# Attention scores: the low part of the rotated queries as 64-row products, two banks of keys side by side

## The chip, the core and the metric

The kernel runs on one core of one Trainium2 chip. The metric is the device time of one execution in microseconds (us). A core has five engines with a queue of their own: TensorE (PE in the profile; its weight loads are listed apart as PEld), VectorE (DVE), ScalarE (ACT), GpSimd (POOL) and SyncE (SP, which issues most DMAs). Products land in PSUM, eight banks of 512 fp32 values on each of 128 partitions.

## The reference

One layer of a hybrid backbone on 2048 latent and 256 context tokens: an input projection feeds latent attention, a bidirectional HGRN2 scan and Fourier mixing; then come an output projection and a SwiGLU FFN. The change is in the attention scores. With absorbed weights, a score of query t and key s is the sum of a 128-long product with the compressed keys and a 64-long product of the rotated parts:

```
q_nope, q_pe = q[..., :MLA_NOPE], q[..., MLA_NOPE:]        # 128 and 64 columns
q_pe = apply_rope(q_pe, rope[0], rope[1])
k = jnp.concatenate([k_nope, jnp.broadcast_to(k_pe, (b, t, MLA_HEADS, MLA_ROPE))], axis=-1)
s = jnp.einsum('bqhd,bkhd->bhqk', qi, k).astype(jnp.float32) * scale
pr = jax.nn.softmax(s, axis=-1).astype(v.dtype)
```

There are 4 heads and 2304 keys.

## The kernel before

Precision is kept by splitting each fp32 operand into a high part (rounded to fp32r, the type that TensorE streams fast) and a low part (the rest). `hi` writes the first, `lo` the second, and `mm3` makes low times high, high times high and high times low in one PSUM bank.

The attention stage lies between about 977 and 1764 us of the span. `group` runs over 4 blocks of 512 queries, 4 heads and 2 halves. One group scores two tiles of 128 queries (I call one such tile with its 2304 keys a unit: 64 units in all) while it gathers the values of the group before: `turn` transposes probabilities (tile `ptv`), ACT and DVE split them into `pth` and `ptl`, and `gather` multiplies them with the compressed keys into `po`. `score_bank(u, j)` makes the scores of 512 keys (256 in the fifth bank, j = 4) in a PSUM tile `sc`, of which there are five. Five products go into each bank:

- `ktl` and `kth` with `q[0]`, and `kth` with `q[1]`: the compressed part, on 128 rows of the array;
- `kp` with `q[2]` and `kp` with `q[3]`: the rotated part. Rows 0 to 63 and 64 to 127 of `q[2]` hold the same 64 rotated values (high part), those of `q[3]` the same low part. `kp` holds the keys' high part on rows 0 to 63 and their low part on rows 64 to 127, so that one 128-row product gives high times both parts.

DVE then takes the maximum of the bank (L890), after the fifth bank the maximum of all (L893), and ACT takes the five exponentials (L896), which free the banks for the next unit. A scheduler sets the order on each engine when the kernel is built; the engines run their queues in that order.

Two other places in the program use a part of the array at a time, and the prediction reads them. In `hgrn` products into `pfin` (L408, L410) use 32 or 64 columns of the array at a `tile_position`. At the start the modulation rows are transposed (L212) with 2 rows, which the compiler places on a tile of 32 rows by 128 columns, and L215 follows on the full array.

Of the kernel before, what the change touches and what calls it, by code (L numbers as in the profile page):

```python
# [14 lines left out]
ALU = mybir.AluOpType  # L15
AX = mybir.AxisListType
# [3 lines left out]
P = 128  # L20
# [4 lines left out]
NTOK = SEQ + CTX  # L25
# [17 lines left out]
def tile_backbone(  # L43
# [6 lines left out]
    pe, act, dve, pool, sp = nc.tensor, nc.scalar, nc.vector, nc.gpsimd, nc.sync  # L50
# [19 lines left out]
    def hi(eng, dst, src):  # L70
        if eng is pool:
            pool.tensor_scalar(dst, src, 1.0, 0.0, ALU.mult, ALU.add)  # L72
        elif eng is act:
            act.copy(dst, src)  # L74
        else:
            dve.tensor_copy(dst, src)

    def lo(dst, src, h, eng=None):
        (eng or dve).tensor_tensor(dst, src, h, ALU.subtract)  # L79
# [548 lines left out]
    with ExitStack() as ph:  # L628
# [16 lines left out]
        kth = cp.tile([P, NTOK], F32R, name="kth")  # L645
        ktl = cp.tile([P, NTOK], F32R, name="ktl")
        kp = cp.tile([P, NTOK], F32R, name="kp")

        def keys(g):

            kv = qp2.tile([P, 2, 256], F32, tag=f"q{g // 2 % 4}", name="kv")
            sp.dma_start(kv, mlap[g // 4][(g % 4) * P:(g % 4 + 2) * P, 256:512].rearrange("(c p) n -> p c n", p=P))
            hi(act, ckh[:, g:g + 2, :], kv[:, :, 0:128])
            lo(ckl[:, g:g + 2, :], kv[:, :, 0:128], ckh[:, g:g + 2, :], pool)
            pt = ps1.tile([P, 512], F32, tag=f"p{'ab'[g // 2 % 2]}{g // 4 % 2}", name="ptk")
            for s in range(2):
                for i in range(2):
                    pe.transpose(pt[:, (2 * s + i) * P:(2 * s + i + 1) * P], kv[:, i, s * P:(s + 1) * P], ident)
            gs = slice(g * P, (g + 2) * P)
            hi(act, kth[:, gs], pt[:, 0:256])  # L660
            lo(ktl[:, gs], pt[:, 0:256], kth[:, gs])
            hi(act, kp[:, gs], pt[:, 256:512])
            lo(kp[64:P, gs], pt[64:P, 256:512], kp[64:P, gs])

        def queries(b):

# [55 lines left out]
        with ExitStack() as early:  # L722
# [34 lines left out]
            for g in (16, 0, 2, 4, 6, 8, 10, 12, 14):  # L757
                keys(g)
# [117 lines left out]
        def score_bank(u, j):  # L876

            q, t = u["q"], u["t"]
            ts = slice(t * P, (t + 1) * P)
            js = slice(j * 512, min((j + 1) * 512, NTOK))  # L880
            n = js.stop - js.start
            if j == 0:
                u["mx"] = rp.tile([P, 16], F32, tag="mx", bufs=4, name="mx")
                u["p"] = b4.tile([P, NTOK], F32, tag="p", name="p")
                u["s"] = []
            s = pss.tile([P, 512], F32, tag="sc", name="sc")
            for i, (a, bb) in enumerate(((q[0], ktl), (q[0], kth), (q[1], kth), (q[2], kp), (q[3], kp))):
                pe.matmul(s[:, :n], a[:, ts], bb[:, js], start=i == 0, stop=i == 4)  # L888
            mx = u["mx"]
            dve.tensor_reduce(mx[:, j:j + 1], s[:, :n], AX.X, ALU.max)  # L890
            u["s"].append(s)
            if j == 4:
                dve.tensor_reduce(mx[:, 5:6], mx[:, 0:5], AX.X, ALU.max, negate=True)  # L893
                for i in range(5):
                    a, e = i * 512, min((i + 1) * 512, NTOK)
                    act.activation(u["p"][:, a:e], u["s"][i][:, :e - a], AF.Exp, bias=mx[:, 5:6],  # L896
                                   accum_out=mx[:, 6 + i:7 + i])
# [78 lines left out]
        def group(cur, prev, tasks):  # L976

            turned = [None] * 9
            for i in range(9 + LAG):
                values = [lambda: gather(prev["po"], prev["g"] * 256, i - LAG, turned[i - LAG])]  # L980
                if prev is None or i < LAG:
                    values = []
                if prev is not None and i < 9:
                    turned[i] = turn(prev["u"], i)
                scores = [lambda: score_bank(cur["u"][i // 5], i % 5)] if cur is not None and i < 10 else []
                for f in values + scores if i % 5 == 0 else scores + values:
                    f()
                if prev is not None and prev["g"] == 1 and i == 3:
                    weights(prev)
                if tasks and i < 10:  # L990
                    more = tasks.pop(0)()
                    if more is not None:
                        tasks.insert(min(2, len(tasks)), more)
            if cur is not None:
                for u in cur["u"]:
                    dve.tensor_reduce(cur["rc"][:, u["t"]:u["t"] + 1], u["mx"][:, 6:11], AX.X, ALU.add)
                if cur["g"] == 1:
                    dve.reciprocal(cur["rc"], cur["rc"])
            if prev is not None and prev["g"] == 1:
                tasks.insert(min(2, len(tasks)), finish(prev["b"], prev["h"], prev["po"], prev["rb"]))  # L1000
# [37 lines left out]
    with ExitStack() as ph:  # L1038
# [90 lines left out]
        gs = ph.enter_context(ExitStack())  # L1129
# [66 lines left out]
        def token_sums(s, k, eng):  # L1196

            raw = raw4("xr")
            for i in range(4):
                sp.dma_start(raw[:, i, :], x2d[s][i][k * P:(k + 1) * P, :])  # L1200
            t = st.tile([P, 3, TB], F32, tag="ws", name="ts")
            block_sums(eng, [raw[:, i, :] for i in range(4)], [t[:, 0, :], t[:, 1, :]], False)
            return raw[:, 0, :], (t[:, 0, :], t[:, 1, :], raw[:, 1, :], raw[:, 2, :])
# [93 lines left out]
        for i, (s, j) in enumerate(units):  # L1297
# [54 lines left out]
            if s == 0 and 2 <= j < 6:  # L1352
                b11, ts = token_sums(1, j - 2, dve)
# [27 lines left out]
        for b in range(NB):  # L1381
            sq = b1.tile([P, 4, 2], F32, tag="sq7", bufs=2, name="sq7")
            rs = b1.tile([P, 4, 2], F32, tag="rs7", bufs=2, name="rs7")
            for c in range(2):
                acc = [bank("dn") for _ in range(4)]
                for g, (k0, nk) in enumerate(DG):
                    i = (b * 2 + c) * len(DG) + g
# [69 lines left out]
```

## Time and profile before

| | |
|---|---|
| time, median of 3 runs | 3330.2 us (3325.0 to 3332.26) |
| profiled execution | 3330.5 us, of which the span is 3328.7 us |
| PE busy | 3167.2 us, 95% of the span, 17034 matmuls |
| DVE, ACT, POOL busy | 2128.5, 951.0, 1029.7 us |
| attention stage (977 to 1764 us) | 787.0 us, PE busy 767.67 us, granted clock 0.99 |

The span runs from the first to the last instruction. Matmuls are pipelined: a row's own duration contains the way through the array, and what one costs in a stream is the distance between the starts of two neighbours.

### The profile page before, as it was taken

The page shows a single profiled execution, that of the slowest core. Times are in us where ns is not written, and L with a number is a line of the kernel's source. Part 1 is how long each engine was busy: PE and PEld are TensorE (multiplying, and loading weights), DVE is VectorE, ACT ScalarE, POOL GpSimd, SP SyncE. Part 2 cuts the span into 40 slices and gives each one's busy share as a digit, 9 for nine tenths or more (in the row PEclk, how much of TensorE's full clock was granted, in tenths as well). Part 3 has the DMA queues.
Part 4 walks back from the last instruction along what each step waited for, and adds up shares of the span by engine and source line. Part 5 has one row for each costly group of instructions (what it writes and reads, how often), then busy time and mean ns, then how long its engine had stood idle before and what let it go on. Part 6 is the DMA issues. An engine that isn't in the chain of part 4 may idle for free. (4 is left out here: it accounts for less than half of the span.)

```text
span 3328.7 us, 45452 instructions
## 1 busy us (share of the span) xinstructions
PE 3167.2 (95%) x17034; PEld 2651.4 (80%) x17034; DVE 2128.5 (64%) x3219; ACT 951.0 (29%) x2028; POOL 1029.7 (31%) x1233
## 2 busy tenths in 40 slices
PE   7998999999889999999999989999999999999998
PEld 5777777777768888888887767888878888888886
DVE  6575665656686767676655467866776666555543
ACT  3323122222335545555552341111121111212111
POOL 3443452424421021121001443333333333243442
PEclk8999999999999999999999999999999999999999
DMA  6523233143361122120106664422342232664552
GB/s 224 170 70 121 81 106 94 55 117 99 117 194 32 45 58 74 52 78 20 52 28 213 232 213 159 139 77 88 109 136 80 77 95 93 211 211 155 177 171 70
DMA packets 354000, 382.03 MB, mean 115 GB/s; under 512 B 46234, under 2 KB 236532, under 8 KB 352756
## 3 DMA queue, kind: packets, MB, share of 16 engines
q1 hardware_dynamic: 339140, 368.11, 35.3%
q10 hardware_dynamic: 13776, 8.92, 0.8%
q8 instruction: 135, 2.21, 0.3%
q0 software_dynamic: 864, 2.10, 0.2%
q14 instruction: 85, 0.70, 0.1%
HBM read 293.33 MB, written 85.72 MB: 114 GB/s over the span
## 5 line engine op out<-in xcount | busy, mean ns | idle before, releaser
L72 POOL TENSOR_SCALAR wp<-wr 128x512 fp32r<-128x512 f32 x208 | 171.3, 837 | 360.9 <-PE dn L85 229.6
L890 DVE TENSOR_REDUCE mx<-sc 128x1 f32<-128x512 f32 (+1 forms) x320 | 201.9, 632 | 121.7 <-PE sc L888 120.8
L85 PE MATMUL dn<-wp,hdl 128*128 128x512 f32 x704 | 274.0, 389 | 0.0
L83 PE MATMUL dn<-wp,hdh 128*128 128x512 f32 x704 | 274.0, 389 | 0.0
L84 PE MATMUL dn<-wp,hdh 128*128 128x512 f32 x704 | 274.0, 389 | 0.0
L79 DVE TENSOR_TENSOR wp<-wr,wp 128x512 fp32r<-128x512 f32 x208 | 171.1, 860 | 138.4 <-POOL wp L72 138.3
L79 DVE TENSOR_TENSOR ptl<-ptv,pth 128x512 fp32r<-128x512 f32 x288 | 196.1, 686 | 67.4 <-ACT pth L74 65.1
L74 ACT CAST pth<-ptv 128x512 fp32r<-128x512 f32 x288 | 169.3, 592 | 239.3 <-PE ptv L904 232.8
L896 ACT ACTIVATE p<-sc,mx 128x512 f32<-128x512 f32 (+1 forms) x320 | 201.6, 648 | 91.0 <-DVE mx L893 87.1
L83 PE MATMUL y<-xol,wp 128*128 128x512 f32 x528 | 208.9, 396 | 12.5 <-ACT e L1309 5.6
L72 POOL TENSOR_SCALAR wp<-wg 128x512 fp32r<-128x512 f32 x176 | 131.7, 749 | 273.5 <-PE y L85 109.5
L84 PE MATMUL y<-xoh,wp 128*128 128x512 f32 x528 | 207.5, 393 | 0.0
L85 PE MATMUL y<-xoh,wp 128*128 128x512 f32 x528 | 206.8, 392 | 0.0
L85 PE MATMUL accf<-xh,wl 128*128 128x512 f32 x448 | 184.8, 412 | 10.4 <-DVE wl L79 10.4
L888 PE MATMUL sc<-kth,q 128*128 128x512 f32 (+1 forms) x640 | 194.5, 377 | 0.0
L79 DVE TENSOR_TENSOR wl<-wraw,wh 128x1536 fp32r<-128x1536 f32 (+3 forms) x78 | 118.6, 1520 | 116.8 <-POOL wh L72 114.0
L888 PE MATMUL sc<-kp,q 128*128 128x512 f32 (+1 forms) x640 | 190.4, 374 | 0.0
L904 PE MATMUL ptv<-ident,p 128*128 128x128 f32 x1152 | 179.5, 275 | 10.2 <-DVE ptl L79 8.7
L83 PE MATMUL accf<-xl,wh 128*128 128x512 f32 x448 | 184.1, 411 | 0.6 <-DVE gt L559 0.5
L79 DVE TENSOR_TENSOR wp<-wg,wp 128x512 fp32r<-128x512 f32 x176 | 129.3, 737 | 86.2 <-POOL wp L72 82.8
L84 PE MATMUL accf<-xh,wh 128*128 128x512 f32 x448 | 183.0, 408 | 0.0
L72 POOL TENSOR_SCALAR wp<-ws 128x512 fp32r<-128x512 f32 x132 | 90.2, 683 | 286.5 <-PE z L85 160.4
(366 smaller groups left out, 8415.0 us busy)
## 6 DMA issues: line engine op xcount, KB each, us to landing
wg<-in_w_gate_up_dram SPq DMA_DIRECT2D x88, 512.0 KB, 4.0
wr<-in_w_down_dram SPq DMA_DIRECT2D x40, 1024.0 KB, 5.1
wraw<-in_w_in_dram SPq DMA_DIRECT2D x112, 256.0 KB, 3.6
hr<-hid SPq DMA_DIRECT2D x88, 256.0 KB, 3.3
wm<-in_w_mod_dram SPq DMA_DIRECT2D x64, 256.0 KB, 2.8
hid<-f SPq DMA_DIRECT2D x44, 256.0 KB, 3.0
hid<-e SPq DMA_DIRECT2D x44, 256.0 KB, 2.0
wt<-in_w_mod_dram SPq DMA_DIRECT2D x8, 1024.0 KB, 7.3
```

The source lines that it names most:

```text
L72: pool.tensor_scalar(dst, src, 1.0, 0.0, ALU.mult, ALU.add)
L74: act.copy(dst, src)
L79: (eng or dve).tensor_tensor(dst, src, h, ALU.subtract)
L83: pe.matmul(ps, ah, bl, start=first, stop=False, skip_group_check=more)
L84: pe.matmul(ps, ah, bh, start=False, stop=False, skip_group_check=more)
L85: pe.matmul(ps, al, bh, start=False, stop=last, skip_group_check=more)
L888: pe.matmul(s[:, :n], a[:, ts], bb[:, js], start=i == 0, stop=i == 4)
L890: dve.tensor_reduce(mx[:, j:j + 1], s[:, :n], AX.X, ALU.max)
L896: act.activation(u["p"][:, a:e], u["s"][i][:, :e - a], AF.Exp, bias=mx[:, 5:6], accum_out=mx[:, 6 + i:7 + i])
L904: pe.transpose(pt[:, i, u * P:(u + 1) * P], ps[u]["p"][:, (2 * g + i) * P:(2 * g + i + 1) * P], ident)
```

## The change

The product of `q[3]` is made on 64 rows of the array, with the keys' high part alone (low times low is left out). The product for an even bank takes rows 0 to 63, that for an odd bank rows 64 to 127. For that `keys` places the keys' high part of odd banks on rows 64 to 127 and the low part on rows 0 to 63. `score_bank` now makes four products per bank; the fifth waits until the second bank of a pair is there, and then the two are issued one behind the other, for banks 0 and 1 and for 2 and 3. Bank 4 (256 keys) has its fifth product alone, on rows 0 to 63. The maxima of a pair are taken behind its two products.

```diff
             hi(act, kp[:, gs], pt[:, 256:512])
-            lo(kp[64:P, gs], pt[64:P, 256:512], kp[64:P, gs])
+            low = slice(64, P) if g // 4 % 2 == 0 else slice(0, 64)
+            lo(kp[low, gs], pt[low, 256:512], kp[low, gs])
...
-            for i, (a, bb) in enumerate(((q[0], ktl), (q[0], kth), (q[1], kth), (q[2], kp), (q[3], kp))):
-                pe.matmul(s[:, :n], a[:, ts], bb[:, js], start=i == 0, stop=i == 4)
+            for i, (a, bb) in enumerate(((q[0], ktl), (q[0], kth), (q[1], kth), (q[2], kp))):
+                pe.matmul(s[:, :n], a[:, ts], bb[:, js], start=i == 0, stop=False)
             mx = u["mx"]
-            dve.tensor_reduce(mx[:, j:j + 1], s[:, :n], AX.X, ALU.max)
             u["s"].append(s)
+            if j % 2 == 0 and j < 4:
+                return
+
+
+            for jj in range(j // 2 * 2, j + 1):
+                ks = slice(0, 64) if jj % 2 == 0 else slice(64, P)
+                js = slice(jj * 512, min((jj + 1) * 512, NTOK))
+                pe.matmul(u["s"][jj][:, :js.stop - js.start], q[3][ks, ts], kp[ks, js], start=False, stop=True,
+                          tile_position=(ks.start, 0))
+            for jj in range(j // 2 * 2, j + 1):
+                dve.tensor_reduce(mx[:, jj:jj + 1], u["s"][jj][:, :min(512, NTOK - jj * 512)], AX.X, ALU.max)
```

PE's queue in the middle of the stage, a unit's fourth and fifth bank, before (`q_10641` to `q_10644` are `q[0]` to `q[3]`):

```order
L888 MATMUL sc<-kp,q_10643 128x512
L888 MATMUL sc<-kp,q_10644 128x512
L83 MATMUL po_10621<-ptl,ckh 128x256
L84 MATMUL po_10621<-pth,ckh 128x256
L85 MATMUL po_10621<-pth,ckl 128x256
L83 MATMUL po_10621<-ptl,ckh 128x256
L84 MATMUL po_10621<-pth,ckh 128x256
L85 MATMUL po_10621<-pth,ckl 128x256
L888 MATMUL sc<-ktl,q_10641 128x256
L888 MATMUL sc<-kth,q_10641 128x256
L888 MATMUL sc<-kth,q_10642 128x256
L888 MATMUL sc<-kp,q_10643 128x256
```

and the same place of the change (`q_10639` to `q_10642` are now `q[0]` to `q[3]`; L889 and L899 are the products on 128 and on 64 rows):

```order
L889 MATMUL sc<-kp,q_10641 128x512
L899 MATMUL sc<-kp,q_10642 128x512 x2
L83 MATMUL po_10621<-ptl,ckh 128x256
...
L889 MATMUL sc<-ktl,q_10639 128x256
L889 MATMUL sc<-kth,q_10639 128x256
L889 MATMUL sc<-kth,q_10640 128x256
L889 MATMUL sc<-kp,q_10641 128x256
L899 MATMUL sc<-kp,q_10642 128x256
L83 MATMUL po_10621<-ptl,ckh 128x256
```

The third bank's fifth product has moved behind the fourth bank's, and 64-row products stand between 128-row products on both sides. Of 128 pairs, 111 stand together like this one.

The other 17 pairs are parted by work on the full array, as here, also on PE's queue, in a unit beside the absorbed queries (`pta`) and the turned rotated queries (`ptp`, L716):

```order
L889 MATMUL sc<-kp,q_10641 128x512
L899 MATMUL sc<-kp,q_10642 128x512
L915 MATMUL ptv<-ident,p 128x128 x4
L899 MATMUL sc<-kp,q_10642 128x512
L716 MATMUL ptp_11263<-ident,qp 128x128 x4
```

Over the whole queue the 64-row products stand in 209 groups: 111 pairs, 34 alone with 512 columns (the 17 parted pairs) and 64 alone with 256 columns (the fifth banks).

DVE's queue, two neighbouring banks of a later unit, before:

```order
L890 TENSOR_REDUCE mx<-sc 128x1
L79 TENSOR_TENSOR ptl<-ptv,pth 128x512 x2
L890 TENSOR_REDUCE mx<-sc 128x1
L79 TENSOR_TENSOR ptl<-ptv,pth 128x512
L890 TENSOR_REDUCE mx<-sc 128x1
L893 TENSOR_REDUCE mx<-mx 128x1
```

and the same place of the change (L902 and L904 are the former L890 and L893):

```order
L79 TENSOR_TENSOR ptl<-ptv,pth 128x512 x2
L902 TENSOR_REDUCE mx<-sc 128x1 x2
L79 TENSOR_TENSOR ptl<-ptv,pth 128x512
L902 TENSOR_REDUCE mx<-sc 128x1
L904 TENSOR_REDUCE mx<-mx 128x1
```

The maximum of a pair's first bank has moved behind the split of probabilities to stand beside that of its second bank.

## Rows read from the trace of the kernel before

**Rows 1.** Page, part 1: busy time, share of the span, instructions of each engine.
```profile
PE 3167.2 (95%) x17034; PEld 2651.4 (80%) x17034; DVE 2128.5 (64%) x3219; ACT 951.0 (29%) x2028; POOL 1029.7 (31%) x1233
```

**Rows 2.** Windows by stage: length, busy time of each engine, granted clock, DMA.
```profile
176.00:977.00 801.00, 730.07 (x4488) 605.86 (x4489) 518.83 (x711) 195.76 (x389) 325.68 (x321) 0.96 0.35 103
977.00:1764.00 787.00, 767.67 (x5022) 678.32 (x5021) 538.37 (x1062) 409.41 (x1011) 98.61 (x149) 0.99 0.19 57
```

**Rows 3.** Waits of PE and its weight loads, 977 to 1764 us: total, times, longest.
```profile
PE ptv L904 <- DVE ptl L79: 8.7, 4, 4.0
...
PEld sc L888 <- ACT p L896: 7.8, 22, 1.8
```

**Rows 4.** Timeline of PE, end of a unit: start, duration, instruction, count.
```profile
1206.93 0.61 PE L888 MATMUL sc<-kp,q 128*128 128x512 f32 x2
1207.38 0.28 PE L83 MATMUL po<-ptl,ckh 128*128 128x256 f32 x1
...
1208.45 0.40 PE L888 MATMUL sc<-kp,q 128*128 128x256 f32 x2
1208.69 0.28 PE L83 MATMUL po<-ptl,ckh 128*128 128x256 f32 x1
```

**Rows 5.** Timeline of PE around the products with 32 and 64 columns of the array.
```profile
887.17 0.39 PE L83 MATMUL accf<-xl,wh 128*128 128x512 f32 x1
887.40 0.40 PE L84 MATMUL accf<-xh,wh 128*128 128x512 f32 x1
887.72 0.22 PE L408 MATMUL pfin<-q,k 128*32 128x32 f32 x1
...
887.99 0.20 PE L410 MATMUL pfin<-q,k 128*32 128x32 f32 x1
888.11 0.50 PE L85 MATMUL accf<-xh,wl 128*128 128x512 f32 x1
888.45 0.39 PE L83 MATMUL accf<-xl,wh 128*128 128x512 f32 x1
...
890.33 0.22 PE L408 MATMUL pfin<-q,k 128*64 128x64 f32 x1
...
890.38 0.22 PE L408 MATMUL pfin<-q,k 128*64 128x64 f32 x1
890.39 0.22 PE L410 MATMUL pfin<-q,k 128*64 128x64 f32 x1
890.54 0.50 PE L83 MATMUL pu<-cwl,zh 128*128 128x512 f32 x1
890.88 0.39 PE L84 MATMUL pu<-cwh,zh 128*128 128x512 f32 x1
```

**Rows 6.** Timeline of PE's weight loads at the same place.
```profile
887.17 0.19 PEld L84 LDWEIGHTS accf<-xh,wh 128*128 128x128 f32 x1
887.72 0.11 PEld L408 LDWEIGHTS pfin<-q,k 128*32 128x32 f32 x1 [0.36 <-issue]
...
888.11 0.19 PEld L85 LDWEIGHTS accf<-xh,wl 128*128 128x128 f32 x1
888.22 0.19 PEld L83 LDWEIGHTS accf<-xl,wh 128*128 128x128 f32 x1
```

**Rows 7.** Timeline of PE, last of eight 2-row products and the first on all rows.
```profile
33.22 0.20 PE L212 MATMUL pmt<-ident,mrow 2*128 2x2 f32 x1
33.34 0.38 PE L215 MATMUL pmt<-ones,macc 128*128 128x1 f32 x2
```

**Rows 8.** Timelines of DVE, ACT and PE from a unit's last maxima to the next unit.
```profile
1207.99 0.68 DVE L890 TENSOR_REDUCE mx<-sc 128x1 f32<-128x512 f32 x1
1208.89 0.42 DVE L890 TENSOR_REDUCE mx<-sc 128x1 f32<-128x256 f32 x1 [0.21 <-PE sc L888]
...
1209.54 0.69 ACT L896 ACTIVATE p<-sc,mx 128x512 f32<-128x512 f32 x1 [2.18 <-DVE mx L893]
...
1210.67 0.48 PE L888 MATMUL sc<-ktl,q 128*128 128x512 f32 x1
```

## The prediction

> **What bounds the kernel now.** I read the busy times first: PE is busy for 95% of the span, the next engine, DVE, for 64% [rows 1]. The windows by stage come next, because the change is in one stage. In attention PE is busy for 767.67 of 787.0 us at a granted clock of 0.99 [rows 2], so only 19 us are left open. The waits say who ends those: the largest names are 8.7 us for DVE's split of the probabilities and 7.8 us for the exponentials that free a score bank [rows 3]. So what PE's queue takes longer or shorter here goes into the time nearly one to one, and the question is what PE's queue costs per product. The timeline gives that as the distance between starts: two neighbouring 512-column products take 0.45 us, 0.225 each, and two with 256 columns take 0.24 us, 0.12 each [rows 4].
>
> **The change, part by part.** *What it removes.* Of 320 fifth products on 128 rows, 256 have 512 columns. If two 64-row products run side by side, each of the 111 pairs that stand together in PE's queue costs one product instead of two: 111 x 0.225 = 25.0 us saved. The 34 alone with 512 columns and the 64 alone with 256 columns save nothing, since a product's distance goes by the columns that it streams, and these stay. Do two tiles run side by side? No 64-row pair is in the trace. The nearest rows are the pairs on two halves of the columns: their starts are at most 0.01 us apart, and the next pair follows after 0.06 us [rows 5]. I take "side by side" for the 64-row pairs; the other end is a pair that costs two products, and gives back the 25.0 us.
>
> *What it adds: a change of the array's division on both sides of each of the 209 groups.* The trace shows what that costs where the kernel divides the array by columns. On the way in, the full-array products at 887.17 and 887.40 are 0.23 us apart, and the second is followed at 887.72, 0.32 us later: 0.09 us lost [rows 5]. Also lost is the cover of the weight load. Between full-array products the next weights load while the last product streams: the load for the product of 887.40 begins at 887.17. The load at 887.72 starts together with its own product [rows 6]. What an uncovered load of 128 weight columns costs is seen on the way out: from the product at 888.11 to the next are 0.34 us instead of 0.23, 0.11 more [rows 5], and its load starts only at 888.11 too [rows 6]. The 64-row products load 128 columns of weights as well, so I charge 0.11 us on the way in and 0.11 us on the way out. The way out itself: the last pair at 890.38 is followed at 890.54, 0.15 to 0.16 us later, where pairs follow each other after 0.05 to 0.06 us [rows 5]: 0.10 us lost.
>
> Together 0.09 + 0.11 + 0.10 + 0.11 = 0.41 us per group. This is priced by columns of the array, and the change divides rows. One place has rows: the last product on 2 rows (a tile of 32 rows) starts at 33.22, and the next one, on the full array, at 33.34 [rows 7]. That is 0.12 us, the same as behind the last 32-column product (887.99 to 888.11) [rows 5]. So on the way out rows cost what columns cost; on the way in nothing but the column case is there, and I take it.
>
> The Trainium skill ("TensorEngine Tiling (Array Packing)", Theoretical Speedup) gives up to 2x for two tiles of 64 rows, by which the sum would be the bare saving, 25.0 us faster. The same page (Key Properties) says that changing the tiling mode, and not merely the tile, drains TensorE, and gives no price; the rows above agree with it and give 0.12 us from last start to next load.
>
> The other edits cost nothing or little. `keys` has as many instructions as before, on other partitions, outside the stage. The second product of a pair starts some 0.01 us behind the first, 1 us in all. DVE has the same maxima; they now stand in pairs. Before, bank 4's maximum began 0.90 us after bank 3's, of which 0.21 us were idle [rows 8]. Two maxima in a row of 0.68 us each can make bank 4's maximum, and with it the exponentials and the freeing of the banks, 0.68 - 0.21 = 0.47 us late. The cover is this: the first exponential ends at 1209.54 + 0.69 = 1210.23, and PE starts the next unit's scores at 1210.67 [rows 8], so 0.44 us are free, and PE is itself later now. I charge nothing; without that cover it would be 64 x 0.47 = 30 us.
>
> *The sum.* 209 x 0.41 = 85.7 us more, 25.0 us less, 60.7 us net. The 26 groups that transposes follow pay a shorter load, some 1 us less in all by my estimate from the 0.11 us. I take +60 us on the profiled execution's 3330.5 us, which is 0.3 us from the median: 3390 us.
>
> **The rivals.** *The other side: no stop for rows.* If rows can be divided and joined while products stream, with weights loaded ahead, only the saving is left: 3330.5 - 25.0 = 3305 us. What decides is the price per group, and the point is 25.0 / 209 = 0.12 us. Against it speaks the 0.12 us from a 32-row tile to the full array, with an uncovered load behind it [rows 7]; for it, that no row shows the way in, and that one place near the start is all there is for rows.
>
> *Half the price.* The stop is there both ways, but weights wait ready behind it: 0.09 + 0.10 per group, 209 x 0.19 = 39.7, less 25.0: +14.7, 3345 us. Or the way in is free and only the way out costs, 0.21 x 209 = 43.9, less 25.0: +18.9, 3349 us. The uncovered load at 888.11 speaks against the first, nothing against the second but the column rows.
>
> *The pair runs one after the other.* The saving falls away: +85.7, 3416 us. Against it speak the column pairs. If only the second tile's weights load behind the first's, 111 x 0.11 = 12 us come on top of the forecast, 3402 us.
>
> *DVE's tail.* Bank 4's maximum comes late and the exponentials with it: up to 30 us on top, 3420 us. It decides once the delay exceeds the 0.44 us of cover.
>
> *The clock.* A PE with more gaps could be granted less. In the stage before, with PE busy 91% of the time, the granted clock was 0.96 against 0.99 here [rows 2]. Between 2.4 and 1.2 GHz, 0.03 of mean clock is 0.06 of the time at half speed, which loses half of it: 0.03 x 850 = 25 us on top, 3415 us.
>
> **How the numbers follow.** Forecast (3370 to 3405 us, the second tile's load included): 0.60. Half the price: 0.10. Pair in sequence: 0.09. DVE's tail: 0.07. Clock: 0.04. No stop: 0.10. The range from 3343 to 3420 us holds the forecast, half the price, the pair in sequence, and a part of the tail and the clock, and leaves out the no-stop case. A difference of 0.2% (7 us) is about what a measurement can tell from none. Only the no-stop case is faster (0.10); 0.02 for a mixture that ends within 7 us; 0.88 slower.
>
> **What would show it.** Each step has its mark in the profile of the changed kernel. Right: 64-row pairs with starts about 0.01 us apart; 0.32 us from a 512-column product to the first of a pair, and 0.21 us from a 256-column one; no 64-row weight load that starts ahead of its product; about 0.42 us from a pair's start to the next load (0.11 uncovered, 0.21 streaming, 0.10 stop), and 0.34 us from the next 512-column product to its follower; a stage of about 847 us. PE's other waits stay below 20 us, and the span outside the stage does not move. Wrong: loads of 64-row tiles that start while the product ahead still streams, 0.23 us into and out of a pair (no stop), starts 0.2 us apart (in sequence), or score products that wait longer for the exponentials (DVE's tail). The prediction fails most easily at the way into the 64-row tiles, which no row of this trace shows.

## The result and the profile after

The change makes the kernel slower: 3373.65 us median (3371.22 to 3379.23, 4 runs) against 3331.23 us (3325.0 to 3334.89, 4 runs), a ratio of 1.0132 with a 95% interval of 1.0119 to 1.0145. That is 42 us more where 60 were forecast. The profiled execution took 3379.23 us with a span of 3377.5 us, the slowest of its four runs.

The page after, its span and part 1, answers to [rows 1]: PE's share is the same 95% of a longer span.

```profile
span 3377.5 us, 45432 instructions
PE 3211.2 (95%) x17034; PEld 2628.3 (78%) x17034; DVE 2130.8 (63%) x3219; ACT 950.9 (28%) x2028; POOL 1027.5 (30%) x1233
```

Where the time went is seen from the first product of each bank. The view of the source line before (L888) and after (L889) says between which starts these 320 products lie; the columns are the shortest, median and longest duration in ns, then first and last start in us.

```profile
L888 PE MATMUL sc<-ktl,q x320: 278/476/799, 976.4 to 1740.0; 128*128 128x512 f32 x128, 128*128 128x256 f32 x32
```
```profile
L889 PE MATMUL sc<-ktl,q x320: 280/476/796, 973.2 to 1782.6; 128*128 128x512 f32 x128, 128*128 128x256 f32 x32
```

Before, 1740.0 - 976.4 = 763.6 us lie between them, after 1782.6 - 973.2 = 809.4 us. The stage has grown by 45.8 us, to some 833 us where about 847 were forecast; the rest of the two profiled spans differs by 3 us (48.8 - 45.8).

The timeline of PE after, at the place of [rows 4], shows a pair (L899, 512 columns) and a fifth bank's product (L899, 256 columns).

```profile
1207.51 0.40 PE L889 MATMUL sc<-kp,q 128*128 128x512 f32 x1
1207.84 0.50 PE L899 MATMUL sc<-kp,q 64*128 64x512 f32 x2
1208.27 0.39 PE L83 MATMUL po<-ptl,ckh 128*128 128x256 f32 x1
1208.49 0.28 PE L84 MATMUL po<-pth,ckh 128*128 128x256 f32 x1
...
1209.88 0.28 PE L889 MATMUL sc<-kp,q 128*128 128x256 f32 x1
1210.09 0.38 PE L899 MATMUL sc<-kp,q 64*128 64x256 f32 x1
1210.40 0.39 PE L83 MATMUL po<-ptl,ckh 128*128 128x256 f32 x1
1210.62 0.28 PE L84 MATMUL po<-pth,ckh 128*128 128x256 f32 x1
```

The two products of the pair together last 0.50 us, as long as one full-array product with an uncovered load (888.11 in [rows 5]), so they run side by side. But 0.33 us pass from the product ahead to the pair, 0.43 from the pair to the next product, and 0.22 from that to its follower: 0.98 us, where three plain 512-column products and one of 256 columns take 3 x 0.225 + 0.12 = 0.80 us. For the fifth bank it is 0.21 + 0.31 + 0.22 = 0.74 us, where three plain 256-column products take 0.36 us.

PE's weight loads at the pair:

```profile
1207.28 0.19 PEld L889 LDWEIGHTS sc<-kp,q 128*128 128x128 f32 x1
1207.83 0.19 PEld L899 LDWEIGHTS sc<-kp,q 64*128 64x128 f32 x2 [0.36 <-issue]
1208.26 0.19 PEld L83 LDWEIGHTS po<-ptl,ckh 128*128 128x128 f32 x1 [0.24 <-issue]
1208.37 0.19 PEld L84 LDWEIGHTS po<-pth,ckh 128*128 128x128 f32 x1
```

The two loads for the pair start together, and only with the pair (1207.83); the load behind it starts with its own product too (1208.26). The next one is ahead of its product again (1208.37 for the product of 1208.49). The bracket names the idle time ahead and what ended it; "issue" means that the profile shows no other engine or transfer behind the wait.

### The profile page after: what moved, and what is told of

Same layout as the page of the kernel before. It is cut to its first block, busy times and chain, and to the rows that moved or that the text cites. A ratio compares the mean times of both kernels' runs of the same rounds, so it can differ in the third digit from the quotient of the medians.

```text
span 3377.5 us, 45432 instructions
## 1 busy us (share of the span) xinstructions
PE 3211.2 (95%) x17034; PEld 2628.3 (78%) x17034; DVE 2130.8 (63%) x3219; ACT 950.9 (28%) x2028; POOL 1027.5 (30%) x1233
## 5 line engine op out<-in xcount | busy, mean ns | idle before, releaser
L902 DVE TENSOR_REDUCE mx<-sc 128x1 f32<-128x512 f32 (+1 forms) x320 | 195.0, 632 | 73.9 <-PE sc L899 71.9
L889 PE MATMUL sc<-kth,q 128*128 128x512 f32 (+1 forms) x640 | 190.0, 376 | 0.0
L83 PE MATMUL po<-ptl,ckh 128*128 128x256 f32 x576 | 181.7, 315 | 0.0
```

What stands on the lines that cost most here:

```text
L83: pe.matmul(ps, ah, bl, start=first, stop=False, skip_group_check=more)
L902: dve.tensor_reduce(mx[:, jj:jj + 1], u["s"][jj][:, :min(512, NTOK - jj * 512)], AX.X, ALU.max)
```

## The experiments

Three theories stood against each other: the changes of the array's division cost (switch theory), the new order of products and maxima costs (order theory), or a 64-row product costs more whatever stands beside it (per-product theory). The last three kernels add a fourth, late maxima at the end of a unit (tail theory). The first four kernels shared runs of the kernel before with a median of 3332.2 us (17 runs), the last three 3330.26 us (17 runs).

**The order alone.**

```diff
-                pe.matmul(u["s"][jj][:, :js.stop - js.start], q[3][ks, ts], kp[ks, js], start=False, stop=True,
-                          tile_position=(ks.start, 0))
+                pe.matmul(u["s"][jj][:, :js.stop - js.start], q[3][:, ts], kp[:, js], start=False, stop=True)
```

> The order of the change with nothing divided: the fifth product of a pair is issued behind the second bank and the maxima stand in pairs, but each product runs on all 128 rows. If the changes of the array's division are what costs (switch theory), this is the kernel before: 3331 us, at most 6 us off. If the order is what costs, by maxima that stand in pairs and exponentials that start late (order theory), it keeps the loss: about 3374 us less what the pairs save side by side, so 3374 + 25 = 3399 us, and at least 3350.

Measured: 3327.76 us median (3322.37 to 3337.97, 12 runs), ratio 0.9989 (0.9979 to 1.0). The same 209 places in PE's queue, the same pairs of maxima, and no loss. The order theory falls; the delayed fifth products and the paired maxima cost nothing that can be measured.

**Both products on the same rows.** The keys keep the layout of before.

```diff
-            low = slice(64, P) if g // 4 % 2 == 0 else slice(0, 64)
-            lo(kp[low, gs], pt[low, 256:512], kp[low, gs])
+            lo(kp[64:P, gs], pt[64:P, 256:512], kp[64:P, gs])
...
-                ks = slice(0, 64) if jj % 2 == 0 else slice(64, P)
+                ks = slice(0, 64)
```

> The change with both products of a pair on rows 0 to 63, one behind the other, so that the 209 groups stay and only the running side by side is taken away. If it saves 111 x 0.227 = 25 us in the change, as the starts 3 ns apart say, this takes 3374 + 25 = 3399 us (3388 to 3402). If two 64-row products share the way into the array and save nothing, it stays at 3374 us.

Measured: 3397.49 us (3395.26 to 3400.25, 4 runs), ratio 1.0196 (1.0183 to 1.0209): 24 us above the change, as the side-by-side saving says. PE's timeline at a pair:

```profile
1210.45 0.39 PE L888 MATMUL sc<-kp,q 128*128 128x512 f32 x1
1210.77 0.73 PE L898 MATMUL sc<-kp,q 64*128 64x512 f32 x2
1211.43 0.50 PE L888 MATMUL sc<-ktl,q 128*128 128x512 f32 x1
```

The pair now lasts 0.73 us instead of 0.50, and from its start to the next product there are 0.66 us instead of 0.43: one plain product more. The way in stays at 0.32 us.

**The fifth bank on the full array.**

```diff
-                pe.matmul(u["s"][jj][:, :js.stop - js.start], q[3][ks, ts], kp[ks, js], start=False, stop=True,
-                          tile_position=(ks.start, 0))
+                if jj == 4:
+                    pe.matmul(u["s"][4][:, :256], q[3][:, ts], kp[:, js], start=False, stop=True)
+                else:
+                    pe.matmul(u["s"][jj], q[3][ks, ts], kp[ks, js], start=False, stop=True, tile_position=(ks.start, 0))
```

> The change with the fifth bank's product on all 128 rows again, so that 145 of 209 groups are left. Switch theory: 64 groups x 0.42 us = 27 us back, less some 5 us of waits elsewhere that return when PE is quicker: 3374 - 27 + 5 = 3352 us (3345 to 3358). Order theory: unchanged at 3374 us, since no maximum moves.

Measured: 3355.3 us (3350.56 to 3357.43, 4 runs), ratio 1.0067 (1.0054 to 1.008). Taking 64 of the 209 groups away gives 18 us back, 0.29 us for each: less than the price of a group, as forecast with the waits that return. One of them has a name: weight loads for the transposes of probabilities that wait for the exponentials. These lines are from the change and from this kernel (waiting in us, times, longest):

```profile
PEld ptv L915 <- ACT p L907: 1.7, 1, 1.7
```
```profile
PEld ptv L917 <- ACT p L909: 8.4, 32, 2.0
```

**The kernel before with each fifth product on 64 rows.** Low times low is left out here too.

```diff
             for i, (a, bb) in enumerate(((q[0], ktl), (q[0], kth), (q[1], kth), (q[2], kp), (q[3], kp))):
-                pe.matmul(s[:, :n], a[:, ts], bb[:, js], start=i == 0, stop=i == 4)
+                if i < 4:
+                    pe.matmul(s[:, :n], a[:, ts], bb[:, js], start=i == 0, stop=False)
+                else:
+                    pe.matmul(s[:, :n], a[0:64, ts], bb[0:64, js], start=False, stop=True, tile_position=(0, 0))
```

> The kernel before with each fifth product on rows 0 to 63 in its old place, so that the order stays and 320 groups of one product arise. Switch theory: 256 x 0.40 + 64 x 0.42 = 129 us more, less some 20 us that waits elsewhere give up: 3331 + 109 = 3440 us (3420 to 3460). If a 64-row product costs more whatever stands beside it (per-product theory: the change's gross 83.6 us over its 320 products, 0.26 us each), 3331 + 84 less 14 = 3401 us. Order theory: 3331 us.

Measured: 3442.54 us (3437.11 to 3446.72, 4 runs), ratio 1.033 (1.0316 to 1.0343): 110 us more, 0.34 us for each of 320 groups. The per-product theory gave 3401 us, the order theory 3331 us; only the switch theory holds. The largest waits of PE's weight loads in this stage are those of the 64-row products, with no engine named:

```profile
PEld sc L891 <- issue: 90.7, 259, 0.7
PEld po L83 <- issue: 26.1, 107, 0.2
```

**Fewer groups: banks 2, 3 and 4 together.** If groups are what costs, fewer and larger ones should pay.

```diff
-            if j % 2 == 0 and j < 4:
+            if j not in (1, 4):
                 return
+            j0 = 0 if j == 1 else 2
...
-            for jj in range(j // 2 * 2, j + 1):
+            for jj in range(j0, j + 1):
...
-            for jj in range(j // 2 * 2, j + 1):
+            for jj in range(j0, j + 1):
```

> The change with the products of banks 2, 3 and 4 in one group behind the fifth bank: 131 groups instead of 209 (61 of three products, 67 pairs, 3 alone), and the maxima of banks 2, 3 and 4 one behind the other at the end of the unit. If only the groups count: 131 x 0.40 = 52 us more, 128 x 0.224 = 29 us less by pairs, some 9 us taken up by waits: 3331 + 14 = 3345 us (3338 to 3354). If the late maxima push the exponentials past their cover (tail theory): bank 4's maximum comes two maxima of 0.68 us later, 1.36 - 0.44 = 0.9 us for each of 64 units, so up to 3345 + 58 = 3403 us, and at least 3365.

Measured: 3381.68 us (3381.27 to 3384.1, 4 runs), ratio 1.0157 (1.0144 to 1.0171). With 78 groups fewer this is slower than the change, and inside what the tail theory gave. The ends of a unit on PE, DVE and ACT:

```profile
1213.21 0.61 PE L900 MATMUL sc<-kp,q 64*128 64x512 f32 x3
1213.75 0.38 PE L83 MATMUL po<-ptl,ckh 128*128 128x256 f32 x1
...
1214.07 1.61 DVE L903 TENSOR_REDUCE mx<-sc 128x1 f32<-128x512 f32 x3
1215.82 0.69 DVE L79 TENSOR_TENSOR ptl<-ptv,pth 128x512 fp32r<-128x512 f32 x1
1216.43 0.15 DVE L905 TENSOR_REDUCE mx<-mx 128x1 f32<-128x5 f32 x1
...
1216.84 0.69 ACT L908 ACTIVATE p<-sc,mx 128x512 f32<-128x512 f32 x1
```

The three products are done when the next one starts at 1213.75. Three maxima and a split stand between them and the maximum of all; the first exponential begins at 1216.84, 3.1 us behind the products. Before, it began 0.85 us behind them (1208.69 to 1209.54) [rows 4, 8]. PE then meets it where it wants to transpose the probabilities; its two largest waits from 970 to 1850 us are

```profile
PE ptv L916 <- ACT p L908: 20.8, 21, 2.8
PE ptr L871 <- POOL sg L866: 11.0, 8, 2.4
```

where before the first was 1.5 us and the second 2.0 us in the stage. The first is the tail theory's. The second names another engine, GpSimd, which makes the gated values `sg` that are transposed into `ptr`; no run shows whether the late maxima hold that up too.

**One group: banks 0 to 3 together, the fifth on the full array.** The product as in the third experiment, and

```diff
-            if j % 2 == 0 and j < 4:
+            if j < 3:
                 return
+            j0 = 0 if j == 3 else 4
...
-            for jj in range(j // 2 * 2, j + 1):
+            for jj in range(j0, j + 1):
...
-            for jj in range(j // 2 * 2, j + 1):
+            for jj in range(j0, j + 1):
```

> Banks 0 to 3 in one group behind the fourth bank, the fifth bank's product on all rows: 72 groups (56 of four products, 16 pairs), the four maxima one behind the other behind the group. If only the groups count: 72 x 0.40 = 29 us more and 128 x 0.224 = 29 us less: 3331 us, or some 5 us below it by waits that are taken up. Tail theory: the fifth bank's maximum begins up to 4 x 0.68 = 2.7 us behind the group, where PE needs about 1.4 us to that bank's end, so 1.3 - 0.44 = 0.9 us late in each of 64 units: up to 3331 + 55 = 3386 us, and at least 3350.

Measured: 3358.22 us (3353.33 to 3359.46, 5 runs), ratio 1.0083 (1.0069 to 1.0098). Again above the count and inside the tail theory's bounds, at about half of its upper end (27 of 55 us). The same two waits stand at the head of the list:

```profile
PE ptv L918 <- ACT p L910: 15.4, 21, 3.2
PE ptr L871 <- POOL sg L866: 13.7, 8, 2.6
```

**One group and early maxima.** The maximum only shifts the exponentials, so it may be taken before the low product is added. The keys lie as in the change; the edit is shown against it.

```diff
-                pe.matmul(s[:, :n], a[:, ts], bb[:, js], start=i == 0, stop=False)
+                pe.matmul(s[:, :n], a[:, ts], bb[:, js], start=i == 0, stop=i == 3)
+            dve.tensor_reduce(mx[:, j:j + 1], s[:, :n], AX.X, ALU.max)
...
-            if j % 2 == 0 and j < 4:
-                return
...
+            if j == 4:
+                for jj in range(5):
+                    ks = slice(0, 64) if jj % 2 == 0 else slice(64, P)
+                    js = slice(jj * 512, min((jj + 1) * 512, NTOK))
+                    pe.matmul(u["s"][jj][:, :js.stop - js.start], q[3][ks, ts], kp[ks, js], start=False, stop=True,
+                              tile_position=(ks.start, 0), skip_group_check=True)
```

> All five 64-row products of a unit behind its fifth bank, and each bank's maximum taken in its old place, before the low product is added (the maximum is only the shift of the exponentials). The scheduler makes 92 groups of it with about 121 pairs. No maximum is late, so both theories agree: 92 x 0.40 = 37 us more, 121 x 0.224 = 27 us less, some 6 us taken up by waits: 3331 + 4 = 3335 us (3327 to 3345). Above 3350 us would say that exponentials that wait for the 64-row products cost of themselves.

Measured: 3328.72 us (3320.49 to 3334.48, 12 runs), ratio 0.9993 (0.9982 to 1.0004). The whole loss of the change is gone, with the 64-row products later than in any other kernel; so late products alone did not cost in the two kernels ahead. The wait of the transposes for the exponentials is down to 0.6 us, and the one for GpSimd to 2.6. How much of the time regained is due to fewer groups (92 instead of 209) and how much to the early maxima stays open: the early maxima with every product on the full array were not run. A group of five on PE:

```profile
1200.33 0.28 PE L889 MATMUL sc<-kp,q 128*128 128x256 f32 x1
1200.54 0.97 PE L897 MATMUL sc<-kp,q 64*128 64x512 f32 x5
1201.43 0.39 PE L83 MATMUL po<-ptl,ckh 128*128 128x256 f32 x1
1201.66 0.28 PE L84 MATMUL po<-pth,ckh 128*128 128x256 f32 x1
```

The way in (0.21 us) and the follower behind (0.23 us) are those of a single product: a group pays once, whatever it holds. From the product ahead to the second one behind, 0.21 + 0.89 + 0.23 = 1.33 us pass; seven plain products there take 4 x 0.225 + 3 x 0.12 = 1.26 us. Five are no gain, and the last one, the fifth bank's, has no partner beside it. Groups of four, two pairs, come out about even: the 56 in the kernel ahead take 0.87 us each (median, with what they add to the distances around them), and four plain products take 4 x 0.227 = 0.91. No version here beats the kernel before by more than can be measured.

## Why the prediction was right, and which term was mis-sized

*What bounds.* PE's queue does. What it costs went into the time, but less nearly one to one than the prediction had it.

*The pairs run side by side.* Right. Over the trace of the change the second product of a pair starts 3 ns behind the first (median of 111), and the kernel that takes this away is 24 us slower, where 25.0 us were worked out.

*The price of a group.* Right. The prediction had 0.09 + 0.11 + 0.10 + 0.11 = 0.41 us, from columns. In the change the median from a 512-column score product to the first of a group is 0.319 us, and from the 256-column one 0.209. From the last of a pair to the next product it is 0.428, and from a next product of 256 columns to its follower 0.223. I summed, over all 209 groups, what these three distances exceed plain ones by (0.227, 0.119 and, for transposes, 0.108 us, as measured in this stage). That gives 83.6 us, 0.40 per group; 85.7 had been worked out. Less 111 x (0.227 - 0.003) = 24.9 us for the pairs, the groups should cost 58.7 us net, close to the 60 forecast. The way in, which no row had shown, is the same for rows as for columns. Transposes follow 27 groups, not 26, which changes nothing here.

*What was mis-sized is a term that the prediction left at zero.* It took the waits elsewhere in the stage as fixed ("what PE's queue takes longer or shorter here goes into the time nearly one to one"). The stage grew by 45.8 us, 13 less than the groups cost. Summed in the same way, PE's distances that do not belong to a group exceed plain ones by 54.4 us before and 41.4 us after. The kernel with the order alone splits this, since it has the same 209 places: 52.3 us in all, 4.8 of them at those places. So 2 us went with the order, 4.8 us were waits and uncovered loads where a group now stands and has paid already, and 6 us are waits elsewhere that a later PE no longer meets, most of them between transposes of probabilities (9.8 us above plain distances with the order alone, 4.5 after). The profile lists this wait by name, in the trace of the kernel before:

```profile
PEld ptv L904 <- ACT p L896: 8.1, 32, 1.7
```

Thirty-two times a weight load for the transposes waits for the exponentials. In the change one such wait of 1.7 us is left; with the fifth bank on the full array the 32 are back. So the groups at the fifth bank stand, in part, where PE waited anyway. The prediction misread the list here: it called the 7.8 us for the score banks one of the two largest names [rows 3], but this wait is larger, and I had not asked which waits shrink when PE is later. The change in the median, 42 us, lies 3 us under the profiled stage's 45.8, within the spread of the runs.

*The rivals.* No stop, half the price and the pair in sequence fall with the rows after. DVE's tail does not show in the change: the order alone, with the same paired maxima, loses nothing. The rival is real all the same: with three or four maxima in a row at the end of a unit the kernels took 3382 and 3358 us, where the forecasts from the count of groups and pairs gave 3345 and 3331. About half of that difference has the tail's name in the list of PE's waits (20.8 and 15.4 us, against 1.5 before). The granted clock in the stage is 0.99 as before:

```profile
977.00:1812.00 835.00, 818.76 (x5040) 662.54 (x5039) 541.04 (x1061) 409.46 (x1012) 99.32 (x150) 0.99 0.18 54
```

*The rule.* The Trainium skill's page "TensorEngine Tiling (Array Packing)" says in Key Properties that changing the tiling mode drains TensorE, and in Theoretical Speedup that a dimension of at most 64 gives up to 2x. The traces agree with the first and price it: beyond the streaming PE loses 0.09 us into a group and 0.10 us out of it, and on both sides about 0.105 us more for a weight load that is not covered. The 2x holds for the two products themselves, which start 3 ns apart, and is lost around them.

## What to carry to other kernels

What dividing the array costs goes by the group, not by the product: here a group costs 0.40 us, and a pair of 512-column products saves 0.224 us, so two such pairs must stand together, with no full-array work in between, to come out about even. Whoever gathers products into larger groups must look at what is queued behind them on the other engines; here three maxima in a row at the end of a unit went with a loss larger than what 78 groups fewer saved, and with four in a row 137 groups fewer brought 15 us, where at 0.40 us each they are worth 55. And a term "PE is busy, so it goes in one to one" should be checked against PE's own small waits, which gave up 13 of 59 us.

## What the runs showed of the hardware that was not expected

- The price of a group does not depend on how many products it holds: the way in is 0.21 us behind a 256-column product for one (the change) and for five (early maxima), and 0.32 us behind a 512-column product for one, two on different rows, and two on the same rows. From the first product behind a group to the next it is 0.22 us for one and 0.23 for five, with 256 columns.
- Inside a group, a load for rows that are in use is hidden. In the kernel with both products on the same rows the pair lasts 0.73 us, one plain product more than the 0.50 us side by side; its two loads together last 0.29 us, from the pair's start:

```profile
1210.77 0.29 PEld L898 LDWEIGHTS sc<-kp,q 64*128 64x128 f32 x2 [0.36 <-issue]
```

- A load of 64 rows by 128 columns takes as long as one of 128 by 128 (0.19 us in the rows after), so half the rows do not make the load shorter.
